# Both merge gates as seven-product groups, with gates and projections behind both attentions, in a two-layer decoder trunk

## The chip, the cores and the metric

The kernel runs on one core of one Trainium2 chip. The metric is the device time of one execution of the whole program, in microseconds (us); lower is better. Engines are named as the profile names them: PE multiplies matrices (PEld is its weight load), DVE is the vector engine, ACT the scalar engine, POOL the GpSimd engine, and SP issues the weight transfers. Three timed executions of the kernel before took 1797.25, 1796.99 and 1792.23 us.

## The reference

Two layers (DEPTH = 2) act on x of 512 tokens by 1024 features, all in float32. Cut to what matters here:

```python
proj = x @ w_in[l]
(r_q, r_k, r_v, r_g, m_qk, m_v, m_o, m_i, m_f, g_a, g_b) = jnp.split(proj, IN_OFFSETS, axis=-1)
o_ret = _head_norm(_retention(rq, rk, rv), ret_norm_g[l]) * jax.nn.silu(r_g.astype(f32))
y_ret = o_ret.astype(dt) @ w_proj_ret[l]
o_ml = _head_norm(_mlstm(mq, mk, mv, i_pre, f_pre), mlstm_norm_g[l]) * jax.nn.sigmoid(m_o.astype(f32))
y_ml = o_ml.astype(dt) @ w_proj_mlstm[l]
gate_a = jax.nn.sigmoid(g_a + b_merge[l, :D_MODEL])
gate_b = jax.nn.sigmoid(g_b + b_merge[l, D_MODEL:])
mix = (gate_a * y_ret + gate_b * y_ml) @ w_out[l]
x = _layer_norm(DEEPNORM_ALPHA * x + mix, ln1_g[l], ln1_b[l])
gu = x @ w_gate_up[l]
hidden = jax.nn.silu(gu[..., :D_FF]) * gu[..., D_FF:]
x = _layer_norm(DEEPNORM_ALPHA * x + hidden @ w_down[l], ln2_g[l], ln2_b[l])
```

The two merge gates, g_a and g_b, are two products of the 512 x 1024 input with 1024 x 1024 weights. The two projections have the same size.

## The kernel before, in words

**Arithmetic.** Every float32 operand is split into a high part and a low part (`whi` and `wlo` of a weight, `x0h` and `x0l` of the input), and every product is made of three matmuls: high x high, high x low, low x high. ACT casts the high part of a weight (`hi_to`, L205), DVE subtracts to get the low part (`lo_of`, L137).

**Weights.** All weights come in units of 128 x 1024 numbers in the order that `layer_plan` (L54) lists. SP loads them into a ring of five raw buffers; the high and low parts have rings of five (`NRING`). After a unit has been used, `used` prepares the units up to four ahead (`LOOK`).

**Units.** A feature unit (`feat`, L270) gives 128 output features for all 512 tokens: 8 blocks of the contraction by 3 parts, 24 matmuls of 512 columns. A token unit (`tok_units`, L359) gives 512 features by blocks of 128 tokens.

**Seven-product groups.** `quad` (L302) computes 2 x 128 output features twice (four units) by Strassen-Winograd: seven products in place of eight, on blocks of half the contraction by half the tokens. A group has 7 x 2 x 4 x 3 = 168 matmuls of 256 columns. It needs four sums of input blocks (tiles `sh`, `sl`; `s0h` in the profile) and four sums of weight blocks (three on DVE in `sum_to`, L191 to L195, one on POOL, L227). The products are called p1, p3, p5, p7, p6, p2, p4, in this order, and go to PSUM banks a, e, c, d (main) and b (auxiliary). Some banks are copied out and then added to again. Before the change only the feed-forward stage uses groups, ten in a layer.

**Order of stages in a layer.** Retention for two pairs of heads; gate A (8 feature units); projection A (8 feature units); mLSTM for two pairs of heads; gate B (8 units); projection B (8 units), mixed with the first branch; output projection; LayerNorm; feed-forward up, then down; LayerNorm.

**Side work.** The attention of a pair of heads (`scores`, `weighted`) and the norm of its outputs (`head_norms`, L515) are generators in the queue `side`. The main stream of matmuls calls `slot` at fixed places, and each call runs one step of the side work, so that small matmuls and transposes stand between large ones. `drain` runs what is left.

**Order on the engines.** PE and SP run in the order in which the code is written. ACT, DVE and POOL are ordered by a scheduler, except in the stretch of the feed-forward groups, where they too follow the code. Every engine runs its own instructions strictly in its order.

**Buffers.** The tag `sc` has four scratch buffers. The tags `qk`, `tab`, `oo`, `vh`, `vl`, `gt`, `pp` hold one tile each at a time. Two pairs of large buffers (`bigpair`) alternate: one holds the layer's input, the other (`oth`) holds the head outputs, `or0h` and `or0l` for retention, then `om0h` and `om0l` for mLSTM (0 is the layer). Projection A's result goes to DRAM (`yd`) and comes back as `ya`.

Of the kernel before, what the change touches and what calls it, by code (L numbers as in the profile page):

```python
# [15 lines left out]
P = 128  # L16
# [37 lines left out]
def layer_plan():  # L54
# [20 lines left out]
    for m in range(8):  # L75
        feat("in", O_GA + m * P)
    for m in range(8):
        feat("ret", m * P)
# [6 lines left out]
    for m in range(8):  # L85
        feat("in", O_GB + m * P)
    for m in range(8):
        feat("ml", m * P)
# [15 lines left out]
QUADS = [layer_plan().index(("F", "gu", j * P)) for j in range(2, FT, 2)]  # L104
# [4 lines left out]
def decoder_trunk(ctx: ExitStack, tc: tile.TileContext, wall, xT_in, x_in, pvec, lnp, rtab, out):  # L109
# [405 lines left out]
    def head_norms(oo, p, gt, gain, oTh, oTl):  # L515
# [22 lines left out]
        for hh in range(2):  # L538
            for f in range(2):
                m = 2 * (2 * p + hh) + f  # L540
# [6 lines left out]
                yield  # L547

# [4 lines left out]
    for l in range(L):  # L553
# [7 lines left out]
        oTh, oTl = bigpair(oth, f"or{l}")  # L561
# [62 lines left out]
        for p in range(2):  # L624
# [29 lines left out]
            side.append(scores(qk, 0, boxes[0], *ret_weights(2 * p)))  # L654
            if p == 0:
                side.append(rest(12))
                side.append(if_cols())
# [28 lines left out]
            side.append(head_norms(oo, p, gt, gain, oTh, oTl))  # L686

        sgs = [reg.tile([P, 4, S], F32, tag="qk", name="sga0"), reg.tile([P, 4, S], F32, tag="tab", name="sga1")]

        def gate_evac(m, base):  # L690
            def ev(pm):
                nc.scalar.activation(sgs[m // 4][:, m % 4], pm, AF.Sigmoid, bias=pv[:, C_BM + base + m : C_BM + base + m + 1])
            return ev

        for m in range(8):
            feat(xh, xl, gate_evac(m, 0))
        drain()
        yd = dr.tile([2, P, 4, S], F32, tag="yd", name="yd")

        def ya_evac(m):  # L700
            def ev(pm):
                s = sgs[m // 4][:, m % 4]
                nc.vector.tensor_tensor(out=s, in0=pm, in1=s, op=ALU.mult)
                if m % 4 == 3:
                    nc.gpsimd.dma_start(yd[m // 4], sgs[m // 4])
            return ev

        for m in range(8):
            feat(oTh, oTl, ya_evac(m))

        oTh, oTl = bigpair(oth, f"om{l}")
# [20 lines left out]
        for p in range(2):  # L732
# [68 lines left out]
            side.append(head_norms(oo, p, gt, gain, oTh, oTl))  # L801


        sgs = [reg.tile([P, 4, S], F32, tag="qk", name="sgb0"), reg.tile([P, 4, S], F32, tag="tab", name="sgb1")]
        for m in range(8):
            feat(xh, xl, gate_evac(m, 8))
        drain()
        yas = [reg.tile([P, 4, S], F32, tag="vh", name="ya0"), reg.tile([P, 4, S], F32, tag="vl", name="ya1")]
        for i in range(2):
            nc.gpsimd.dma_start(yas[i], yd[i])  # L810
        xr = []
        for b in range(NB):
# [3 lines left out]
        gb = reg.tile([P, 2, DM], F32, tag="pp", name="gb1")  # L816
        nc.gpsimd.dma_start(gb, lnp[l, 0:2].unsqueeze(0).broadcast_to([P, 2, DM]))
        mxh, mxl = bigpair(cur, f"mx{l}")

        def mix_evac(m):  # L820
            def ev(pm):
                s = sgs[m // 4][:, m % 4]
# [6 lines left out]
        for m in range(8):  # L829
            feat(oTh, oTl, mix_evac(m))  # L830
# [293 lines left out]
```

## Time and profile before

| | |
|---|---|
| three timed executions | 1797.25, 1796.99, 1792.23 us (median 1796.99) |
| the profiled execution, its own time | 1793.49 us |
| its span in the profile | 1791.8 us |
| mean granted PE clock | 0.998 |
| bytes moved by DMA | 200.95 MB, 112 GB/s on average |
| gate stages of layer 0 in the trace | gate A about 172.6 to 216.1 us, gate B about 414.5 to 458 us |
| feed-forward groups of layer 0 in the trace | 572.6 to 774 us |

The profile is of one execution. Its page lists the busy time of each engine, the span in 40 equal slices with a digit for the busy share, the DMA queues, the chain of work that ended last, and the costliest groups of instructions. From the trace behind it come further views: busy time by stretch of time, instructions in order of time, groups by line, and who waited for whom. A matmul's listed duration includes the time to drain, so matmuls overlap in the list; what one costs in a stream is the distance from its start to the next start. The lines that the argument uses stand with it below.

### The profile page before, as it was taken

What the parts mean: (1) busy time and instruction counts of PE and PEld (TensorE: products, weight loads), DVE (VectorE), ACT (ScalarE), POOL (GpSimd) and SP (SyncE); (2) the same over time, 40 slices, a digit from 0 to 9 for tenths busy, and PEclk for the clock granted to TensorE, in tenths of its full rate; (3) what the DMA queues carried; (4) which work ended last, traced back from release to release, by engine and by line L of the source; (5) the groups of instructions that cost most, each with busy time, mean ns of one, the idle gap of its engine ahead of it and who ended that gap; (6) DMA issues with size and microseconds to landing.
All of it is one profiled execution on the core that took longest, in us unless ns stands there. A gap on an engine that the chain in (4) does not pass through costs nothing.

```text
span 1791.8 us, 24875 instructions
## 1 busy us (share of the span) xinstructions
PE 1778.2 (99%) x10040; PEld 1559.8 (87%) x10040; DVE 1144.4 (64%) x1582; ACT 741.9 (41%) x1056; POOL 327.9 (18%) x245
## 2 busy tenths in 40 slices
PE   9999999999999999999999999999999999999998
PEld 7888888888889999988898888888888899999886
DVE  6665236664459999963476542467535599999534
ACT  4435326554316444451244343256442254444410
POOL 2020000010001455620120100010000015554200
PEclk9999999999999999999999999999999999999999
DMA  7322343234332333363242222522442232333621
GB/s 248 94 83 71 95 148 111 83 115 167 95 95 89 124 95 99 105 216 98 83 165 85 92 82 88 167 87 71 141 153 94 95 107 95 107 115 105 205 71 47
DMA packets 65267, 200.95 MB, mean 112 GB/s; under 512 B 6232, under 2 KB 8152, under 8 KB 63104
## 3 DMA queue, kind: packets, MB, share of 16 engines
q1 hardware_dynamic: 58768, 168.32, 29.3%
q0 software_dynamic: 6384, 31.04, 4.9%
q8 instruction: 79, 1.29, 0.3%
q14 instruction: 36, 0.29, 0.1%
HBM read 186.73 MB, written 12.60 MB: 111 GB/s over the span
## 4 chain that ended last, share of the span: by engine, by line
PE 97%; DVE 1%; ACT 0%; issue 0%; DMA 0%; SPq 0%; DVEq 0%
PE pm L322 19%; PE pm L264 10%; PE pm L266 10%; PE pm L265 10%; PE pm L355 9%; PE pm L357 9%; PE pm L356 9%; PE pa L322 3%; PE pa L356 3%; PE pa L355 3%; PE pa L357 3%; PE pa L488 1%; PE pa L489 1%; PE pa L490 1%; PE pa L543 1%; PE pa L462 1%
## 5 line engine op out<-in xcount | busy, mean ns | idle before, releaser
L137 DVE TENSOR_TENSOR wlo<-wraw,whi 128x1024 fp32r<-128x1024 f32 (+2 forms) x380 | 533.2, 1414 | 347.1 <-ACT whi L205 344.3
L205 ACT CAST whi<-wraw 128x1024 fp32r<-128x1024 f32 x367 | 384.5, 1050 | 616.1 <-PE pm L265 224.8
L444 POOL TENSOR_TENSOR rs<-ve,nhalf 128x4 f32<-128x4 f32 (+1 forms) x32 | 32.1, 1003 | 643.7 <-DVE ve L443 643.7
L264 PE MATMUL pm<-x20h,whi 128*128 128x512 f32 (+1 forms) x288 | 106.9, 371 | 0.0
L266 PE MATMUL pm<-x20h,wlo 128*128 128x512 f32 (+1 forms) x288 | 105.4, 366 | 0.0
L265 PE MATMUL pm<-x20l,whi 128*128 128x512 f32 (+1 forms) x288 | 105.3, 366 | 0.0
L355 PE MATMUL pm<-whi,x0h 128*128 128x512 f32 x256 | 102.3, 400 | 1.8 <-DVE rvl L137 1.7
L355 PE MATMUL pm<-whi,x20h 128*128 128x512 f32 x256 | 102.3, 400 | 0.6 <-DVE rvl L137 0.6
L357 PE MATMUL pm<-wlo,x20h 128*128 128x512 f32 x256 | 100.3, 392 | 0.0
L357 PE MATMUL pm<-wlo,x0h 128*128 128x512 f32 x256 | 100.3, 392 | 0.0
L356 PE MATMUL pm<-whi,x20l 128*128 128x512 f32 x256 | 100.0, 391 | 0.0
L356 PE MATMUL pm<-whi,x0l 128*128 128x512 f32 x256 | 100.0, 391 | 0.0
L264 PE MATMUL pm<-x0h,whi 128*128 128x512 f32 x232 | 91.8, 396 | 0.0
L266 PE MATMUL pm<-x0h,wlo 128*128 128x512 f32 x232 | 90.4, 390 | 0.0
L265 PE MATMUL pm<-x0l,whi 128*128 128x512 f32 x232 | 90.3, 389 | 0.0
L975 POOL TENSOR_TENSOR qa<-qa 128x512 f32<-128x512 f32 x20 | 42.8, 2140 | 142.6 <-DVE qa L974 90.6
L322 PE MATMUL pm<-x10h,whi 128*128 128x256 f32 x240 | 67.9, 283 | 0.0
L322 PE MATMUL pm<-x10l,whi 128*128 128x256 f32 x240 | 67.9, 283 | 0.0
L322 PE MATMUL pm<-s0h,whi 128*128 128x256 f32 x240 | 67.9, 283 | 0.0
L322 PE MATMUL pm<-s0l,whi 128*128 128x256 f32 x240 | 67.9, 283 | 0.0
L322 PE MATMUL pm<-s0h,wlo 128*128 128x256 f32 x240 | 67.9, 283 | 0.0
L322 PE MATMUL pm<-x11h,whi 128*128 128x256 f32 x240 | 67.9, 283 | 0.0
(452 smaller groups left out, 4969.2 us busy)
## 6 DMA issues: line engine op xcount, KB each, us to landing
wraw<-wall SPq DMA_DIRECT2D x307, 512.0 KB, 3.6
yd<-sga POOLq DMA_DIRECT2D x4, 1024.0 KB, 5.0
ya<-yd POOLq DMA_DIRECT2D x4, 1024.0 KB, 6.1
gb<-lnp POOLq DMA_DIRECT2D x4, 1024.0 KB, 5.1
x1d<-xr POOLq DMA_DIRECT2D x8, 512.0 KB, 3.0
xr<-x1d POOLq DMA_DIRECT2D x8, 512.0 KB, 4.6
negm<-md POOLq DMA_DIRECT2D x2, 1026.0 KB, 6.7
xr<-xtok POOLq DMA_DIRECT2D x4, 512.0 KB, 4.0
```

Of the source, the lines that this page charges most:

```text
L137: nc.vector.tensor_tensor(out=out_lo, in0=full, in1=hi.bitcast(F32), op=ALU.subtract)
L205: nc.scalar.copy(hi, sum_t[i])
L264: nc.tensor.matmul(pm[:, c0:c1], lhsT=hi[:, k], rhs=xh[:, k, c0:c1], start=(k == 0), stop=False)
L265: nc.tensor.matmul(pm[:, c0:c1], lhsT=hi[:, k], rhs=xl[:, k, c0:c1], start=False, stop=False)
L266: nc.tensor.matmul(pm[:, c0:c1], lhsT=lo[:, k], rhs=xh[:, k, c0:c1], start=False, stop=(k == KT - 1))
L322: nc.tensor.matmul(pm, lhsT=x[:, j, k], rhs=y[:, k], start=go and n == 0, stop=j == 1 and k == 3 and n == 2, skip_group_check=not first)
L355: nc.tensor.matmul(pm, lhsT=sh(k)[:, a], rhs=hi[:, j], start=first, stop=False)
L356: nc.tensor.matmul(pm, lhsT=sl(k)[:, a], rhs=hi[:, j], start=False, stop=False)
L357: nc.tensor.matmul(pm, lhsT=sh(k)[:, a], rhs=lo[:, j], start=False, stop=last)
L444: nc.gpsimd.tensor_tensor(out=rs[:, :n], in0=ve[:, :n], in1=nhalf[:, :n], op=ALU.pow)
L462: nc.tensor.matmul(pa[:, :HC], lhsT=k[:, t0:t1], rhs=q[:, t0:t2], start=True, stop=True)
L975: nc.gpsimd.tensor_tensor(out=v, in0=v, in1=u, op=ALU.subtract)
```

## The change

It has five parts.

1. **The gates become groups.** Each gate stage is two groups (`quad`) in place of eight feature units. `gate_ev` takes the products out of the banks. Inside the stretch of the four gate groups ACT, DVE and POOL follow the order of the code.
2. **The order of stages** becomes retention, mLSTM, gate A, gate B, projection A, projection B with the mix. `layer_plan` lists the weights accordingly.
3. **Head outputs go through DRAM.** `head_norms` scales a head's two transposed blocks on ACT into a scratch tile `ot`, without splitting it, and POOL's queue stores it to `od`. `fetch`, side work, loads the four blocks of 128 x 1024 later, casts the high part on ACT (`orh`, `om0h`) and subtracts the low part on DVE (`orl`, `om0l`). The retention outputs are fetched during gate B's groups, the mLSTM outputs during projection A.
4. **The four input sums** of the groups (`xs0h`, `xs0l`) are made once per layer by `input_sums`, as side work of the second retention pair, and kept in the large buffers that held the head outputs.
5. **`yd` and `ya` are gone**; gate A's tiles are multiplied by projection A's result in place and stay in SBUF. The `gb1` load follows projection B.

The diff, cut to its core:

```diff
+QUADS = [layer_plan().index(("F", w, c + j * P)) for w, c, js in (("in", O_GA, (0, 4)), ("in", O_GB, (0, 4)),
+                                                                  ("gu", 0, range(2, FT, 2))) for j in js]
...
-    def head_norms(oo, p, gt, gain, oTh, oTl):
+    def head_norms(oo, p, gt, gain, od):
...
+            m = 2 * (2 * p + hh)
+            t = scratch([P, 2, S], "ot")
             for f in range(2):
...
-                nc.scalar.activation(oTh[:, m], pa, AF.Copy, scale=gain[:, m : m + 1])
-                nc.vector.scalar_tensor_tensor(out=oTl[:, m], in0=pa, scalar=gain[:, m : m + 1],
-                                               in1=oTh[:, m].bitcast(F32), op0=ALU.mult, op1=ALU.subtract)
+                nc.scalar.activation(t[:, f], pa, AF.Copy, scale=gain[:, m + f : m + f + 1])
                 yield
+            nc.gpsimd.dma_start(od[:, m : m + 2], t)
+            yield
+
+    def fetch(od, his, los):
+        for i in range(4):
+            t = scratch([P, 2, S], "of")
+            nc.gpsimd.dma_start(t, od[:, 2 * i : 2 * i + 2])
+            yield
+            yield
+            hi, lo = (x[i // 2][:, 2 * i % 4 : 2 * i % 4 + 2] for x in (his, los))
+            nc.scalar.copy(hi, t)
+            yield
+            lo_of(lo, t, hi)
+            yield
+
+    def input_sums(xh, xl, sh, sl):
+        t1, t2 = slice(0, S // 2), slice(S // 2, S)
+        for m in range(4):
+            t = scratch([P, 2, S], "xs")
+            for i in range(2):
+                nc.gpsimd.tensor_tensor(out=t[:, i], in0=xh[:, m + 4 * i].bitcast(F32), in1=xl[:, m + 4 * i].bitcast(F32), op=ALU.add)
+            yield
...
+            nc.scalar.copy(sh[:, :, m], f)
+            lo_of(sl[:, :, m], f, sh[:, :, m])
+            yield
...
+        def gate_ev(sg, base, m):
...
+            def ev(name, banks):
+                two = lambda n: t.setdefault(n, scratch([P, 2, S], n))
+                if name == "p1":
+                    nc.scalar.copy(two("ga")[:, 0], banks["a"])
+                elif name == "p5":
+                    nc.scalar.copy(two("ga")[:, 1], banks["c"])
+                elif name == "p7":
+                    nc.vector.tensor_tensor(out=two("gc")[:, 1], in0=t["ga"][:, 1], in1=banks["d"], op=ALU.subtract)
+                elif name == "p6":
+                    u, v = t["ga"][:, 0], t["ga"][:, 1]
+                    nc.vector.tensor_tensor(out=u, in0=banks["b"], in1=u, op=ALU.add)
+                    nc.gpsimd.tensor_tensor(out=v, in0=v, in1=u, op=ALU.subtract)
+                    nc.gpsimd.tensor_tensor(out=t["gc"][:, 1], in0=t["gc"][:, 1], in1=u, op=ALU.subtract)
+                elif name == "p2":
+                    sigmoid(banks["a"], 0, 0)
+                    nc.vector.tensor_tensor(out=t["gc"][:, 0], in0=banks["e"], in1=t["ga"][:, 1], op=ALU.add)
+                elif name == "p4":
+                    nc.vector.tensor_tensor(out=t["ga"][:, 1], in0=banks["d"], in1=t["ga"][:, 0], op=ALU.add)
...
+        with tc.manual_schedule(engines=ordered):
+            for m in (0, 4):
+                quad(xh, xl, *xs, gate_ev(sga, 0, m))
+            drain()
+            orh = [reg.tile([P, 4, S], F32R, tag=t, name="orh") for t in ("vh", "vl")]
+            orl = [reg.tile([P, 4, S], F32R, tag=t, name="orl") for t in ("gt", "oo")]
+            side.append(fetch(od[0], orh, orl))
+            for m in (0, 4):
+                quad(xh, xl, *xs, gate_ev(sgb, 8, m))
+            drain()
...
+        omh, oml = bigpair(oth, f"om{l}")
+        side.append(fetch(od[1], [omh[:, :4], omh[:, 4:]], [oml[:, :4], oml[:, 4:]]))
         for m in range(8):
+            feat(Halves(orh), Halves(orl), ya_evac(m))
```

How the order of instructions changes, at three places of layer 0. Line numbers of the changed kernel are some lines off from those of the kernel before, as the diff inserts and removes lines.

PE, start of gate A. Before, one feature unit is 24 matmuls of 512 columns with the input as moving operand:

```order
L264 MATMUL pm<-x0h,whi 128x512
L265 MATMUL pm<-x0l,whi 128x512
L266 MATMUL pm<-x0h,wlo 128x512
L264 MATMUL pm<-x0h,whi 128x512
L265 MATMUL pm<-x0l,whi 128x512
L266 MATMUL pm<-x0h,wlo 128x512
```

With the change, the last token unit of the mLSTM (L353) is followed by the first product of a group, of 256 columns each:

```order
L353 MATMUL pm<-wlo,x0h 128x512
L318 MATMUL pm<-x0h,whi 128x256
L318 MATMUL pm<-x0l,whi 128x256
L318 MATMUL pm<-x0h,wlo 128x256
L318 MATMUL pm<-x0h,whi 128x256
L318 MATMUL pm<-x0l,whi 128x256
L318 MATMUL pm<-x0h,wlo 128x256
```

The matmuls have half the columns, and a stage has 336 of them in place of 192.

ACT, first group of gate B in the changed kernel: `ga` holds products taken from a bank, L201 is the cast of a weight's high part, `of` is a fetched block of the head outputs.

```order
L839 COPY ga<-pm 128x512
L201 CAST whi<-wraw 128x1024
L554 CAST orh<-of 128x1024
L201 CAST whi<-wraw 128x1024
L841 COPY ga<-pm 128x512
L201 CAST whi<-wraw 128x1024
L554 CAST orh<-of 128x1024
L201 CAST whi<-wraw 128x1024 x2
L554 CAST orh<-of 128x1024
L833 ACTIVATE sgb<-pm,pv_98 128x256 x2
```

The casts of fetched blocks stand between the casts of weights and the copies out of banks; before, gate B had no such casts, and one sigmoid per unit stood between the weight casts.

POOL, the same place and the second group: L223 is the sum of weight blocks, L847 and L848 combine products, L550 are the loads of head outputs.

```order
L223 TENSOR_TENSOR wraw<-wraw 128x1024
L550 DMA of<-od 128x1024 x3
L847 TENSOR_TENSOR ga<-ga 128x512
L848 TENSOR_TENSOR gc<-gc,ga 128x512
L550 DMA of<-od 128x1024
L223 TENSOR_TENSOR wraw<-wraw 128x1024
L550 DMA of<-od 128x1024 x2
L847 TENSOR_TENSOR ga<-ga 128x512
L848 TENSOR_TENSOR gc<-gc,ga 128x512
L550 DMA of<-od 128x1024 x2
```

The first load stands right behind the sum of weight blocks of the first group, and the fourth behind the two combining operations; the mLSTM outputs' loads follow in the second group.

More of the change, by code (lines that the diff above doesn't have):

```diff
@@ L84, in layer_plan @@
         tok("in", O_MO + p * 512, k8)
[L85 to L88, printed above, removed]
+    for w, col in (("in", O_GA), ("in", O_GB), ("ret", 0), ("ml", 0)):
+        for m in range(8):
+            feat(w, col + m * P)
     for c in range(2):
@@ L560, in decoder_trunk @@
             nc.gpsimd.dma_start(tab, rtab)
-        oTh, oTl = bigpair(oth, f"or{l}")
+        xs = sum_views(oth, f"xs{l}")
+        od = [dr.tile([P, KT, S], F32, tag=f"od{i}", name="od") for i in range(2)]
         def rot_evac(dst):
@@ L685, in decoder_trunk @@
             gain = pv[:, C_RG : C_RG + 8]
[L686 to L711, printed above, removed]
+            side.append(head_norms(oo, p, gt, gain, od[0]))
         negm = reg.tile([P, NH, S + 1], F32, tag="tab", name="negm")
@@ L800, in decoder_trunk @@
             gain = pv[:, C_MG : C_MG + 8]
-            side.append(head_norms(oo, p, gt, gain, oTh, oTl))
-        sgs = [reg.tile([P, 4, S], F32, tag="qk", name="sgb0"), reg.tile([P, 4, S], F32, tag="tab", name="sgb1")]
+            side.append(head_norms(oo, p, gt, gain, od[1]))
+        tab = reg.tile([P, 6, S], F32, tag="tab", name="sg_tab")
+        sga0, sgb0 = reg.tile([P, 4, S], F32, tag="qk", name="sga"), reg.tile([P, 6, S], F32, tag="pp", name="sgb")
+        sga = [(sga0[:, m] if m < 4 else tab[:, m - 4]) for m in range(8)]
@@ L983, in quad_ev @@
             return ev
[L985 removed]
+        with tc.manual_schedule(engines=ordered):
             for j in range(2, FT, 2):
```

56 lines of the change are left out of this document (39 added, 17 removed).

## The prediction

> **What bounds the kernel now.** I read the page first: busy times, slices, and the chain that ended last.
>
> ```profile
> PE 1778.2 (99%) x10040; PEld 1559.8 (87%) x10040; DVE 1144.4 (64%) x1582; ACT 741.9 (41%) x1056; POOL 327.9 (18%) x245
> ...
> PE   9999999999999999999999999999999999999998
> ...
> DVE  6665236664459999963476542467535599999534
> ...
> PEclk9999999999999999999999999999999999999999
> ...
> PE 97%; DVE 1%; ACT 0%; issue 0%; DMA 0%; SPq 0%; DVEq 0%
> ```
>
> PE is busy in every slice, its clock is granted in full, and 97% of the last chain is PE. Of 1791.8 us it is idle for 13.6, mostly at the two ends. So a stage costs the number of its matmuls by the distance between their starts, and the change can win only by that sum. The second thing to see is DVE: it averages 64%, but fills whole slices in the feed-forward groups, and the change puts more such groups into the layer.
>
> Next, who PE waited for:
>
> ```profile
> PE pm L355 <- DVE rvl L137: 2.3, 2, 1.7
> PE pm L399 <- DVE nhalf L401: 1.1, 1, 1.1
> ```
>
> 2.3 us in two waits behind the first attention and 1.1 us at the start: nothing there to win, and any new wait shows at once.
>
> Distances come from the chain in order of time, first for feature units (projection A), then for feed-forward groups:
>
> ```profile
> 204.92 0.23 PE pm L265
> ...
> 207.64 0.23 PE pm L265
> ...
> 572.75 11.52 PE pm L322 x96
> 584.27 2.88 PE pa L322 x24
> 587.15 17.28 PE pm L322 x144
> ```
>
> L265 comes once in three matmuls, and between these two rows it is four threes: 2.72 us / 12 = 0.2267 us for 512 columns. In groups, 11.52 / 96 = 0.1200 us for 256 columns. Half the columns cost 0.53 of the time, not half.
>
> **The change part by part.**
>
> *Gates as groups.* Before, four units take 4 x 24 x 0.2267 = 21.76 us. A group takes 168 x 0.1200 = 20.16 us. One eighth of the products goes, but the smaller matmuls take back half of that, and 1.60 us is left. Two gates in two layers are eight groups: **-12.8 us**. The side transposes that stood between gate units stand between products now, in the same number.
>
> Trainium skill, "TensorE: Matmul & The Clock Gate", section Back-to-back issue gap: a lone warm matmul is followed by the next after its columns / 2.4 plus 2.5 ns, that is 216 ns for 512 columns and 109 ns for 256. By that estimate a group would win 2.4 us and eight would win 19. Both rows above are longer, by 11 ns each, and the same 11 ns on 168 matmuls cost more than on 96; the measured rows decide, so this is not given a chance.
>
> *Retention outputs as moving operand.* They are read from other buffers now: high parts from `vh` and `vl`, low parts from `gt` and `oo`. Tiles of those tags are matmul operands in the down projection:
>
> ```profile
> L264 PE MATMUL pm<-or0h,whi 128*128 128x512 f32 x64 | 24.9, 389 | 0.0
> ...
> L355 PE MATMUL pm<-whi,hd_gt 128*128 128x512 f32 x16 | 6.5, 405 | 0.0
> ...
> L357 PE MATMUL pm<-wlo,hd_oo 128*128 128x512 f32 x16 | 6.3, 391 | 0.0
> ```
>
> Same shape, 2 to 16 ns longer, but there the tile is the stationary operand. For 2 x 192 matmuls in projection A, 0 ns (the present 389) to 6 ns (the common difference) makes 0 to 2.3 us. I take 4 ns, **+1.5 us**.
>
> *Order of stages.* The gates between retention and mLSTM used to give DVE and ACT a rest. The norm of retention's second pair now falls on the mLSTM's first convolution. The trace has that pairing, the first mLSTM pair's norm on the second convolution:
>
> ```profile
> 345.00:358.00 13.00, 13.00 (x67) 10.78 (x66) 10.97 (x16) 6.66 (x10) 0.00 (x0) 1.00 0.36 117
> ```
>
> PE is busy for 13.00 of 13.00 us with DVE at 10.97. The norm also loses its DVE subtraction (L545). Cost nothing; if that cover fails, about the 2.3 us of waits that the first attention has.
>
> *Input sums.* Eight POOL additions of some 2.1 us and their DVE, ACT work lie in the second retention pair, 150 us before their use. Nothing. `yd`, `ya`, `od`: a transfer in DRAM more or less is hidden, except where an engine waits for it in its order, which comes now.
>
> *Gate groups on DVE.* The timeline of one feed-forward group, which starts on PE at 653.2 us (DVE, POOL, ACT):
>
> ```profile
> 655.62 7.58 DVE L137 TENSOR_TENSOR wlo<-wraw,whi 128x1024 fp32r<-128x1024 f32 x3
> ...
> 666.69 1.22 DVE L137 TENSOR_TENSOR wlo<-wraw,whi 128x1024 fp32r<-128x1024 f32 x1
> ...
> 671.81 0.68 DVE L979 TENSOR_TENSOR qb<-pm,qa 128x512 f32<-128x512 f32 x1
> ```
>
> ```profile
> 655.23 2.41 POOL L227 TENSOR_TENSOR wraw<-wraw 128x1024 f32<-128x1024 f32 x1 [2.35 <-issue]
> 657.59 4.53 POOL L957 TENSOR_TENSOR hf_gt<-qb,qc 128x512 f32<-128x512 f32 x2
> ```
>
> ```profile
> 592.90:754.20 161.30, 161.30 (x1347) 161.30 (x1346) 155.90 (x114) 75.28 (x89) 89.09 (x40) 1.00 0.34 105
> ```
>
> DVE is busy 155.9 / 8 = 19.5 us of each 20.16. A subtraction takes 1.22 us alone; three beside 6.94 us of POOL work take 7.58, so DVE loses about (7.58 - 3.66) / 6.94 = 0.56 us per us of POOL. A gate group lacks the POOL products (4.53), so it has about 19.5 - 2.5 = 17.0 us of DVE.
>
> In gate A's first group the norm's work joins: for the second head four statistics, and eight multiplications.
>
> ```profile
> L529 DVE SCALAR_TENSOR_TENSOR moo<-moo,mv,mgt 128x256 f32<-128x256 f32 x32 | 15.1, 476 | 1.4 <-ACT mgt L796 1.4
> L521 DVE BATCH_NORM_STATS2 st<-moo 128x6 f32<-128x256 f32 x32 | 13.2, 422 | 9.4 <-ACT moo L786 9.4
> ```
>
> 4 x 0.42 + 8 x 0.48 = 5.5 us, early, where four weight units lie prepared and no bank is due for DVE until p7 ends at 4 x 2.88 = 11.5 us. With four subtractions (4.9, beside POOL 6.2) DVE is done at about 11.7. Nothing.
>
> In gate B the fetch joins: four casts on ACT, four subtractions on DVE, each in order. The loads are of 512 KB from DRAM, like this one:
>
> ```profile
> xr<-x1d POOLq DMA_DIRECT2D x8, 512.0 KB, 4.6
> ```
>
> The first stands on POOL's queue behind the sum L227, which ends 4.4 us into a group (655.23 + 2.41 - 653.2); landed 4.6 later, 9.0. Until then ACT stands at the cast (1.05 us, as for a weight of that size) and DVE at its subtraction. DVE has had one weight to do by then, until about 4.7, and goes on at 10.05: **5.3 us lost**. Queued behind it are the weights of p2 and p4 and the copies out of the banks. The weights still come in time: p2 starts at 14.4, its low part follows the fetched one at 10.05 + 1.22 + 1.22 = 12.5. The banks don't: the last one from DVE in a group (bank e, at p2) is now free at 19.3 (671.81 + 0.68 - 653.2), and PE needs it in the next group's p3, at 20.16 + 2.88 = 23.0: 3.7 us of slack. Up to there DVE is later by 5.3 + 3 x 1.22 = 9.0, less the 2.5 us of POOL contention and 0.7 us of idle time: 5.8. So PE waits 5.8 - 3.7 = **2.1 us a layer**, +4.2 in two. Bounds: nothing, if the load lands 2 us earlier; 7 us a layer, if a second load holds DVE for its whole 4.6 us and more.
>
> In gate B's second group DVE catches up: no weight sums follow there, 3 x 1.22 less.
>
> Trainium skill, "SBUF — State Buffer", section Who interferes with whom: DVE with two SBUF inputs and a GpSimd read exclude each other for a whole instruction. The rows agree in direction, not in size: 3.9 us are lost beside 6.9. By full exclusion the two POOL operations of p6, 4.4 us, would cost DVE 4.4 in place of 2.5 us, and the wait would be 2 us longer in each layer. The rows' share is in the sum.
>
> **Sum.** -12.8 + 1.5 + 4.2 = -7.1 us, against the profiled execution's own 1793.49 us (span 1791.8 and 1.7 around it): 1786.4. The runs shown have their median 3.5 us above that execution, and all four average 1795.0, 1.5 above. I put the forecast there: **1788.0 us**.
>
> **Rivals.**
>
> *No wait in gate B.* For it: the lead of four prepared units, and feed-forward groups run with PE at 161.30 of 161.30. Against it: the queue places above. With projection A at 389 ns, -12.8: about 1781.
>
> *A second load waits in full.* The third and the fourth stand behind work that itself waits for DVE. 4.6 us and 0.6 of issue more in each layer, +10.4: -7.1 + 10.4 = +3.3, about 1797: no change.
>
> *Every fetched block holds ACT and DVE (slower).* The place is the same, the mechanism is order: the next load can only be issued when a scratch buffer comes free, buffers come free when DVE subtracts, and DVE waits for the load before. Three more waits of 5.2 us in each layer are 31 us: 1786.4 + 31 = 1817.5. For it: `sc` has four buffers and `ga`, `gc` need two of them. Against it: the first two loads are issued together, so each has two buffers to turn in. It decides slower from a wait of 8.4 us a layer: 2 x 8.4 + 1.5 - 12.8 = +5.5.
>
> That the change doesn't do what it says is out: the groups stand on PE, 1344 matmuls of 256 columns in place of 768.
>
> **How the numbers follow.** Forecast 0.50, no wait 0.25, a second load 0.15, every block 0.10. The range leaves out the last alone and takes the bounds: from -12.8 on the fastest run, 1792.23, so 1779.5, to the second load with the four executions' average, 1795.0 + 3.3, so 1798.5. About 0.3% is what a measurement of this kernel can tell from no change, 5.4 us. The forecast crosses that line when the wait exceeds 3 us a layer; I give a third of its chance to that, 0.17. Faster: 0.33 + 0.25 = 0.58. Same: 0.17 + 0.15 = 0.32. Slower: 0.10.
>
> **What would show it.** Gate groups of 20.16 us on PE, with one gap in each layer: at the start of gate B's second group, before its first or second product, ended by DVE or ACT. ACT idle before the first cast of `orh` until a DMA, some 4 us. Projection A's matmuls at 389 to 395 ns. No PE idle time in gate A or the mLSTM's first convolution. Wrong would be: several idle stretches of ACT before `orh` or `om0h` for a DMA, PE waiting in gate A for the norms, or distances in the gate groups off 0.120 us.

## The result, and the profile after

| | before | changed kernel |
|---|---|---|
| executions | 1797.25, 1796.99, 1792.23, 1796.80 us | 1806.10, 1805.87, 1808.64, 1808.35 us |
| median | 1796.89 us | 1807.22 us |
| ratio, 95% interval | | 1.0064 (1.0044 to 1.0083) |
| profiled execution, span | 1793.49 us, 1791.8 us | 1806.10 us, 1804.4 us |

The change makes the kernel slower by 0.64%, outside the predicted range of 1779.5 to 1798.5 us. The page of the changed kernel: busy times, slices of PE, DVE and PE's clock, and the chain that ended last.

```profile
PE 1772.4 (98%) x10616; PEld 1580.5 (88%) x10616; DVE 1263.8 (70%) x1686; ACT 794.3 (44%) x1148; POOL 420.6 (23%) x309
...
PE   9998999999999999999999999999999999999997
...
DVE  6676666775459999963476856667755599999534
...
PEclk9999999999999999999999999999999999999999
...
PE 92%; DVE 5%; issue 1%; ACT 1%; DMA 1%; POOL 0%; SPq 0%; DVEq 0%; ACTq 0%
```

PE is busy for 5.8 us less than before, and yet the span is 12.6 us longer: PE's idle time grew by 18.4 us. One slice of PE is down to 8, the fourth, 135 to 180 us; the chain now holds 5% of DVE. The waits of PE (what PE ran next, whom it waited for, us in total, times, longest):

```profile
PE pm L351 <- DVE rvl L133: 15.1, 4, 6.4
PE pa L318 <- DVE wlo L133: 2.8, 2, 1.7
```

The first row had 2.3 us in two waits before. Now it has 15.1 in four. L351 is a token unit, and `rvl` is the low part of retention's values that DVE copies out of PSUM. The second row is new: gate groups (L318) that wait for a weight's low part.

All stages were compared by the starts of their first matmuls. (By these starts gate A of the kernel before runs from 170.7 to 216.1 us and gate B from 413.6 to 459.0, so each begins one to two us earlier than the table ahead of the prediction says.) A values stage here holds retention's values and its output gates. The ledger of the span, in us:

| where | before | changed | difference, both layers |
|---|---|---|---|
| start, to the first feature unit | 26.42 | 27.45 | +1.0 |
| second values stage of retention, layers 0 and 1 | 54.29, 54.29 | 62.26, 63.26 | **+16.9** |
| gates A and B with the convolution that took a norm over, without waits | 45.41 + 45.39 + 21.76 | 82.37 + 23.65 | -13.1 |
| waits in gate B | 0 | 1.31, 2.38 | +3.7 |
| projection A, each layer | 43.52 | 44.53 | +2.0 |
| down projection of layer 1 to the end of the span | 129.26 | 131.12 | +1.9 |
| the rest | | | +0.2 |
| sum | | | 12.6 |

(82.37 us is what two gate stages take in the run with the longer lead below, where PE does not wait.) In the chain in order of time, a gate group on PE is 24 x 7 matmuls of 0.1200 us, as forecast, until the last group of gate B:

```profile
372.04 17.28 PE pm L318 x144
389.32 2.88 PE pa L318 x24
392.20 17.29 PE pm L318 x144
409.50 1.23 DVE wlo L133
410.77 2.90 PE pa L318 x22
```

Here 17.28 + 2.88 = 20.16 us is one group, and 409.50 is the wait, at the group's fifth product (p6).

**The large term.** Windows of the changed kernel (busy PE, PEld, DVE, ACT, POOL, each with its instructions, then PE's granted clock, DMA share, GB/s). First the values stage up to PE's stop, the stop, and the matmuls behind it:

```profile
117.50:140.60 23.10, 23.10 (x106) 19.21 (x105) 22.61 (x29) 7.20 (x10) 14.46 (x9) 1.00 0.22 71
140.60:147.40 6.80, 0.42 (x3) 0.01 (x1) 6.80 (x11) 4.96 (x7) 0.00 (x0) 0.72 0.36 98
...
147.39:150.11 2.72, 2.72 (x6) 2.14 (x7) 2.72 (x4) 0.97 (x2) 0.00 (x0) 0.50 0.36 142
```

The same stretch before the change:

```profile
116.40:139.30 22.90, 22.90 (x105) 19.01 (x104) 11.80 (x20) 7.81 (x12) 2.32 (x1) 1.00 0.33 108
```

DVE went from 11.80 to 22.61 us, full, and stays full in the next 6.80 us, for 6.38 of which PE stands. The groups of DVE and POOL between 117.5 and 147.4 us (busy, mean ns, idle before):

```profile
L583 DVE TENSOR_TENSOR sf<-xs 128x256 f32<-128x256 f32 x8 | 6.5, 825 | 0.0
L133 DVE TENSOR_TENSOR xs0l<-sf,xs0h 128x1024 fp32r<-128x1024 f32 x4 | 6.0, 1494 | 0.0
L583 DVE TENSOR_TENSOR sf<-sf,xs 128x256 f32<-128x256 f32 x8 | 5.5, 689 | 0.1
...
L577 POOL TENSOR_TENSOR xs<-x0h,x0l 128x512 f32<-128x512 f32 x8 | 12.2, 1539 | 5.5 <-DVE sf L583 2.6 <-DVE xs0l L133 2.0 <-DVE pp L133 0.8
```

These are the input sums: 18.0 us of DVE. What PE needs stands behind them, as DVE's timeline shows:

```profile
138.60 1.51 DVE L583 TENSOR_TENSOR sf<-sf,xs 128x256 f32<-128x256 f32 x1
140.04 0.41 DVE L583 TENSOR_TENSOR sf<-xs 128x256 f32<-128x256 f32 x1
...
145.50 1.23 DVE L133 TENSOR_TENSOR xs0l<-sf,xs0h 128x1024 fp32r<-128x1024 f32 x1
146.65 1.88 DVE L133 TENSOR_TENSOR rvl<-pm,rvh 128x512 fp32r<-128x512 f32 x3
```

```profile
147.39 0.79 PE L351 MATMUL pm<-whi,x0h 128*128 128x512 f32 x1 [6.38 <-DVE rvl L133]
```

The four main banks hold the values until `rvl` has been read out of them, and the gate units of retention that follow need those banks. The copies wait in DVE's order for the last sum, which ends at about 146.7. The row at 138.60 shows the other half: a subtraction that takes 0.41 us alone takes 1.51 beside an addition on POOL.

### The profile page after: what moved, and what is told of

Its sections match the earlier page's. It is cut to its first block, busy times and chain, and to the rows that moved or that the text cites. A ratio compares the mean times of both kernels' runs of the same rounds, so it can differ in the third digit from the quotient of the medians.

```text
span 1804.4 us, 26440 instructions
## 1 busy us (share of the span) xinstructions
PE 1772.4 (98%) x10616; PEld 1580.5 (88%) x10616; DVE 1263.8 (70%) x1686; ACT 794.3 (44%) x1148; POOL 420.6 (23%) x309
## 4 chain that ended last, share of the span: by engine, by line
PE 92%; DVE 5%; issue 1%; ACT 1%; DMA 1%; POOL 0%; SPq 0%; DVEq 0%; ACTq 0%
PE pm L318 25%; PE pm L351 9%; PE pm L352 8%; PE pm L353 8%; PE pm L262 7%; PE pm L260 7%; PE pm L261 7%; PE pa L318 4%; PE pa L352 3%; PE pa L351 3%; PE pa L353 3%; DVE wlo L133 1%; DVE sf L583 1%; PE pa L484 1%; PE pa L485 1%; PE pa L486 1%
## 5 line engine op out<-in xcount | busy, mean ns | idle before, releaser
L133 DVE TENSOR_TENSOR wlo<-wraw,whi 128x1024 fp32r<-128x1024 f32 (+2 forms) x404 | 569.8, 1423 | 231.3 <-ACT whi L201 228.8
L201 ACT CAST whi<-wraw 128x1024 fp32r<-128x1024 f32 x391 | 408.8, 1049 | 507.2 <-PE pm L261 133.9
L351 PE MATMUL pm<-whi,x0h 128*128 128x512 f32 x256 | 102.9, 402 | 8.2 <-DVE rvl L133 8.1
L351 PE MATMUL pm<-whi,x20h 128*128 128x512 f32 x256 | 103.2, 403 | 7.0 <-DVE rvl L133 7.0
L353 PE MATMUL pm<-wlo,x20h 128*128 128x512 f32 x256 | 100.9, 394 | 0.0
L353 PE MATMUL pm<-wlo,x0h 128*128 128x512 f32 x256 | 100.7, 393 | 0.0
L223 POOL TENSOR_TENSOR wraw<-wraw 128x1024 f32<-128x1024 f32 x28 | 67.4, 2408 | 110.1 <-issue 54.4
L318 PE MATMUL pm<-s1h,wlo 128*128 128x256 f32 x240 | 67.9, 283 | 0.0
L318 PE MATMUL pm<-x10h,whi 128*128 128x256 f32 x240 | 67.9, 283 | 0.0
L318 PE MATMUL pm<-x10h,wlo 128*128 128x256 f32 x240 | 67.9, 283 | 0.0
L318 PE MATMUL pm<-s0h,whi 128*128 128x256 f32 x240 | 67.9, 283 | 0.0
L318 PE MATMUL pm<-x11h,whi 128*128 128x256 f32 x240 | 67.9, 283 | 0.0
L318 PE MATMUL pm<-x10l,whi 128*128 128x256 f32 x240 | 67.9, 283 | 0.0
L318 PE MATMUL pm<-s0l,whi 128*128 128x256 f32 x240 | 67.9, 283 | 0.0
L318 PE MATMUL pm<-x11l,whi 128*128 128x256 f32 x240 | 67.9, 283 | 0.0
L318 PE MATMUL pm<-s1h,whi 128*128 128x256 f32 x240 | 67.9, 283 | 0.0
L318 PE MATMUL pm<-s0h,wlo 128*128 128x256 f32 x240 | 67.9, 283 | 0.0
L318 PE MATMUL pm<-x11h,wlo 128*128 128x256 f32 x240 | 67.9, 283 | 0.0
```

What stands on the lines that cost most here:

```text
L133: nc.vector.tensor_tensor(out=out_lo, in0=full, in1=hi.bitcast(F32), op=ALU.subtract)
L201: nc.scalar.copy(hi, sum_t[i])
L223: nc.gpsimd.tensor_tensor(out=raw_t[u + 2], in0=raw_t[u], in1=raw_t[u + 3], op=ALU.add)
L318: nc.tensor.matmul(pm, lhsT=x[:, j, k], rhs=y[:, k], start=go and n == 0, stop=j == 1 and k == 3 and n == 2, skip_group_check=not first)
L351: nc.tensor.matmul(pm, lhsT=sh(k)[:, a], rhs=hi[:, j], start=first, stop=False)
L353: nc.tensor.matmul(pm, lhsT=sh(k)[:, a], rhs=lo[:, j], start=False, stop=last)
```

## The experiments

Ratios are against the kernel before on the same chip: 1796.89 us for the changed kernel, medians of 1794.08 and 1793.85 us in the two sets of experiments. The last two rows have one execution each, and the kernel before had one beside them, of 1793.42 us; for them the time stands in place of the ratio, and only their stages are used. Stage lengths, from the starts of their first matmuls in the profiled executions, in us, layers 0 and 1:

| | ratio (95%) | values stage | two gate stages | projection A | down, layer 0 | down, layer 1, to the end |
|---|---|---|---|---|---|---|
| changed kernel | 1.0064 (1.0044 to 1.0083) | 62.26, 63.26 | 83.68, 84.75 | 44.53 | 122.98 | 131.12 |
| sums of high parts | 0.9967 (0.9954 to 0.9980) | 54.25, 54.25 | 83.81, 85.05 | 44.53 | 122.98 | 131.12 |
| sums spread | 0.9959 (0.9944 to 0.9974) | 54.23, 54.23 | 83.62, 84.48 | 44.53 | 122.98 | 131.12 |
| longer lead | 1.0041 (1.0026 to 1.0056) | 63.63, 63.01 | 82.37, 82.36 | 44.53 | 122.98 | 131.12 |
| padding to 128 B | 1.0038 (1.0023 to 1.0052) | 62.10, 62.28 | 83.59, 84.79 | 44.30 | 122.41 | 130.66 |
| spread and lead | 0.9955 (0.9942 to 0.9967) | 54.23, 54.23 | 82.38, 82.38 | 44.53 | 122.98 | 131.12 |
| and padding to 256 B | 0.9926 (0.9914 to 0.9938) | 54.07, 54.07 | 82.36, 82.36 | 43.55 | 121.51 | 129.64 |
| and stores by SP | 0.9911 (0.9897 to 0.9924) | 54.07, 54.07 | 82.36, 82.36 | 43.55 | 121.51 | 128.35 |
| before, padding to 256 B | 0.9975 (0.9966 to 0.9985) | 54.13, 54.13 | | 43.52 | 121.51 | 127.78 |
| spread, lead of first block | 1803.16 us | 54.23, 54.23 | 91.94, 91.35 | 44.53 | 122.98 | 131.13 |
| spread, lead of last block | 1784.08 us | 54.23, 54.23 | 82.38, 83.19 | 44.53 | 122.98 | 131.13 |

### Sums without POOL's additions

```diff
-            t = scratch([P, 2, S], "xs")
-            for i in range(2):
-                nc.gpsimd.tensor_tensor(out=t[:, i], in0=xh[:, m + 4 * i].bitcast(F32), in1=xl[:, m + 4 * i].bitcast(F32), op=ALU.add)
...
-            a11, a12, a21, a22 = t[:, 0, t1], t[:, 1, t1], t[:, 0, t2], t[:, 1, t2]
+            a11, a12, a21, a22 = (xh[:, m + 4 * i, h].bitcast(F32) for h in (t1, t2) for i in range(2))
```

> The input sums are made from the high parts of the input alone: POOL's eight additions per layer go, DVE's subtractions, ACT's casts and their places stay (the result loses the low part of the input in the summed blocks). Theory LOAD: in the second retention pair the sums are 18.0 us of DVE, 6.4 us of it stretched by POOL's additions; without them DVE has 11.8 + 11.6 = 23.4 us to do in a stage of 23, so PE's wait behind the v units falls from 6.5 us to at most 1 us in each layer, no half-clock matmuls follow, and the time is 1790 to 1794 us. Theory ORDER: the sums stand ahead of the copies out of the v banks on ACT and DVE, each cast waiting for a subtraction, and that chain sets the wait whatever POOL does: a wait of 3.5 us or more stays in each layer and the time is 1799 us or more.

Measured 1788.82 us, ratio 0.9967, a little under the 1790 to 1794 us that LOAD gave; the values stages are back at 54.25. The window and DVE's two groups of sums in it:

```profile
116.82:139.72 22.90, 22.90 (x106) 19.03 (x105) 21.35 (x40) 11.72 (x16) 2.31 (x1) 1.00 0.36 113
...
L580 DVE TENSOR_TENSOR sf<-sf,x0h 128x256 f32<-128x256 f32 x8 | 3.3, 415 | 0.0
L580 DVE TENSOR_TENSOR sf<-x0h 128x256 f32<-128x256 f32 x8 | 3.2, 414 | 0.0
```

The same sixteen instructions, all still ahead of the copies out of the banks, take 6.5 us in place of 12.0, and DVE just fits, with 21.35 of 22.90 us. So the place in the queue alone is not the cause; ORDER falls. The sums and POOL's part in stretching them together overfill the stage.

### Sums spread over four stages

```diff
-            if p == 1:
-                side.append(input_sums(xh, xl, *xs))
...
-            side.append(rest(2))
+            side.append(input_sums(xh, xl, *xs, [p]))
...
-            side.append(rest(2))
+            side.append(input_sums(xh, xl, *xs, [2 + p]))
```

(The first replaced `rest(2)` is in retention's stage of the output gates, the second in the mLSTM's; the new argument lists the blocks to sum.)

> The same sums, a quarter in each of the four stages with gate units of the attentions (31 us each, DVE busy 17 of 31 there before) in place of the two empty steps of the side work. Theory LOAD: some 4.5 us of DVE more per stage fits; no PE wait in any attention, stage lengths as in the kernel before; the 8.0 and 9.0 us that the second retention pair's v stage has over the kernel before go: 1807.2 - 16.9 = 1790.3 us, range 1788 to 1794. Rival PLACE: additions on POOL hurt wherever they stand (the norms' small POOL operations and DVE's chain wait behind them): PE waits of 1 us or more in several of the eight stages, 1797 us or more.

Measured 1787.44 us, ratio 0.9959; LOAD's 1788 to 1794 us were worked out from the first set of runs, in which the kernel before was 2.8 us slower. All the work is done, POOL's too, and no stage is longer for it. This version is faster than the kernel before: what the gates win is real, and the sums hid it.

### A longer lead for the fetched blocks

```diff
-            yield
-            yield
+            for _ in range(4):
+                yield
```

> Only the fetch is changed: four steps in place of two lie between a block's load and its cast. Theory LANDING: ACT and DVE stand 3.0 and 4.3 us for the first fetched block in gate B, and that lag comes out as PE's wait in p6 of gate B's second group (1.2 us in layer 0, 1.9 in layer 1, with 0.4 at its second group's start); with the lead these go: 3.4 us less, 1803.8 us (1802 to 1805.5), ACT's idle time for a DMA before orh under 0.5 us. Rival AMOUNT: gate B has 17 + 5 = 22 us of DVE per 20.16 us group, and the wait stays within 0.7 us in each layer: 1806 to 1808 us.

Measured 1802.56 us, ratio 1.0041, and both gate stages at 82.4. DVE's two waits in gate B of layer 0, in the changed kernel:

```profile
387.47 1.23 DVE L133 TENSOR_TENSOR orl<-of,orh 128x1024 fp32r<-128x1024 f32 x1 [4.34 <-ACT orh L554]
...
408.36 1.23 DVE L133 TENSOR_TENSOR orl<-of,orh 128x1024 fp32r<-128x1024 f32 x1 [3.02 <-ACT orh L554]
```

With the lead:

```profile
388.17 1.23 DVE L133 TENSOR_TENSOR orl<-of,orh 128x1024 fp32r<-128x1024 f32 x1 [2.78 <-ACT orh L554]
...
413.58 1.22 DVE L133 TENSOR_TENSOR orl<-of,orh 128x1024 fp32r<-128x1024 f32 x1
```

The idle time at the first block falls from 4.34 to 2.78 us and that at the fourth from 3.02 to nothing; 1.20 us now stand before the third. PE's wait is gone. The fourth block comes late in the changed kernel for a reason that POOL's timeline shows: its load stands behind the combining of products.

```profile
396.85 4.42 POOL L847 TENSOR_TENSOR ga<-ga 128x512 f32<-128x512 f32 x1 [7.33 <-ACT whi L201]
401.23 1.29 POOL L848 TENSOR_TENSOR gc<-gc,ga 128x512 f32<-128x512 f32 x1
402.46 0.56 POOL L550 DMA_DIRECT2D of<-od  x1
```

LANDING holds in time and stages, though ACT still stands 1.73 us before the first cast of `orh`, where it had given under 0.5. This run does not tell which block PE felt. The last two runs do.

### Padding to 128 B

```diff
-    NPP = O_ST + 2 * (DV + 2)
+    NPP = O_ST + 2 * (DV + 2) + 28
...
-            vh = reg.tile([P, NB, 2, DV + 2], F32R, tag="vh", name="mvh")
+            vh = reg.tile([P, NB, 2, DV + 4], F32R, tag="vh", name="mvh")
```

(`vl` likewise; `weighted` reads as many columns as before.)

> Only padding: mLSTM's v tiles 64 bytes longer, the attention's work tile 112 bytes longer, so that the tiles that share these buffers (orh, orl, hd_vl, hd_gt, the v tiles) all start 96 bytes past a multiple of 128, as x0h and s0h do; before, vl started at 32 and gt at 0. Theory ADDRESS: projection A's 5.3 ns per matmul over 226.7 come from mixing starts; its stage returns from 44.53 to 43.5 us (2.0 us in two layers), and the down projection, 528 matmuls in 122.98 us, comes to about 120 us (528 x 0.2267 = 119.7): 5 to 6 us in two layers; 1798 to 1801 us in all. Rival SWITCH: the extra time comes with every change of operand tile, wherever it starts: no stage changes by more than 0.2 us, 1806 to 1808.5 us.

Measured 1801.63 us, ratio 1.0038. Neither theory fits: projection A went from 44.53 to 44.30, not to 43.5. One tile did move all the way, `pp`, before and after the padding:

```profile
L351 PE MATMUL pm<-whi,hd_pp 128*128 128x512 f32 x24 | 9.5, 396 | 0.0
```

```profile
L351 PE MATMUL pm<-whi,hd_pp 128*128 128x512 f32 x24 | 9.3, 389 | 0.0
```

Its start had moved by 128 B, to a multiple of 256 B from the start of the weight ring; `vl` and `gt` had moved by 64 and 224 B, to 128 and 384 B off, and stayed slow. (The tiles' starts follow from their sizes in the kernel.) So the next padding went to 256 B.

### Both mends together

> The changed kernel with the input sums a quarter at a time in the four stages of the output gates (as in the run that spread them) and with four steps in place of two between the load and the cast of a fetched block (as in the run with the longer lead). LANDING says that the wait in gate B comes from ACT and DVE standing at a block that has not landed, and that it does not depend on what the sums did before: the two gate stages, 83.62 and 84.48 us from the first to the last PE start in the run that only spread, come to 82.4 each as in the run that only had the lead, 3.3 us together, so the span goes from 1785.0 to 1781.7 and the ratio from 0.9959 to about 0.9940. DVE-LIMIT says that the gate groups are short of DVE time whatever the lead, and that the lead helped only because DVE stood elsewhere in that run: the stages stay at 83.5 or more, no ratio under 0.9955.

Measured 1785.00 us, ratio 0.9955: the stages are those that LANDING gives, 82.38 both. The ratio is not the 0.9940 that was worked out from the stages, and its interval meets that of the spread alone; this profiled execution spent 4.0 us more than the spread run's ahead of its second stage of feature units (95.98 against 91.93 us). That is the granted clock: here it was 0.50 from 12.22 to 19.04 and from 63.42 to 66.83 us, with 9.5 us of PE work in these stretches; in the spread run's execution it was 1.00 from 4.72 us until behind the last matmul. The last section shows the second stretch.

### Padding to 256 B

```diff
-    NPP = O_ST + 2 * (DV + 2)
+    NPP = O_ST + 2 * (DV + 2) + 60
...
-            vh = reg.tile([P, NB, 2, DV + 2], F32R, tag="vh", name="mvh")
+            vh = reg.tile([P, NB, 2, DV + 8], F32R, tag="vh", name="mvh")
```

> The kernel before this one in the list, with padding behind the mLSTM's values (6 more elements for each head and block) and behind the table of its weights (60 elements), so that all tiles that feed a matmul start a multiple of 256 B from each other. In the run that padded to 128 B, 227 ns between matmuls came with the tiles whose distance from the weight ring is a multiple of 256 B (pp, which the padding had moved by 128 B, and vh), 231 to 239 ns with those at 64, 128, 160 or 384 B off a multiple. STEP-256 says the residue decides: projection A goes from 44.53 to about 43.6 us in each layer (2 x 0.95), the down projection of layer 0 from 122.98 to about 120.5 (2 x 2.4 in both layers), the attention stages lose some 0.1 us each as before; 6 to 8 us in all, span about 1775. TRAFFIC says that it is what other engines and transfers do in SBUF at that time: projection A stays above 44.2, the down projection above 122.2, and the span falls by no more than the 2.8 us of the padding to 128 B.

Measured 1781.20 us, ratio 0.9926, span 6.3 us less. Projection A's groups in the changed kernel and here (mean ns last but one):

```profile
L261 PE MATMUL pm<-orl,whi 128*128 128x512 f32 x128 | 50.6, 395 | 0.0
L260 PE MATMUL pm<-orh,whi 128*128 128x512 f32 x128 | 50.5, 394 | 0.0
```

```profile
L261 PE MATMUL pm<-orl,whi 128*128 128x512 f32 x128 | 49.8, 389 | 0.0
L260 PE MATMUL pm<-orh,whi 128*128 128x512 f32 x128 | 49.8, 389 | 0.0
```

Projection A is at 43.55, as fast as the projection that reads the old buffers. STEP-256 holds there in full. The down projection lost 1.47 us and not the 2.4 that were expected, but its matmuls too now follow each other at 226 to 228 ns, whatever tile they read: 528 x 0.2267 = 119.7 us, and the other 1.8 us are 16 transposes that stand between them at 0.11 us each. The expectation had left these out.

### The same padding on the kernel before

> The kernel before the change with the padding to 256 B alone. STEP-256 says that its down projections (121.0 to 123 us) lose some 2.4 us each and its attention stages 0.1 us each: 5 to 6 us, ratio about 0.997, with no change in the projections on retention's outputs, which read tiles that stand right already. TRAFFIC says no more than 0.999 to 1.001.

Measured 1788.39 us, ratio 0.9975: both down projections lose 1.47 us, the attention stages 0.1 to 0.2 each. TRAFFIC's 0.999 to 1.001 is out. So 0.25% of the best version's gain belongs to the padding and not to the change; with the padding in both, change and mends make 1781.20 / 1788.39 = 0.9960.

### The end of the program

```diff
-            nc.gpsimd.dma_start(od[:, m : m + 2], t)
+            nc.sync.dma_start(od[:, m : m + 2], t)
```

> The kernel before this one in the list, with the 16 stores of the head outputs issued on SyncE's queue in place of POOL's. The program ends with a drain on POOL, which took 5.04 us in the kernel before with 49 transfers issued on POOL and 7.00 us in the changed one with 73; it ends last of all engines there. DRAIN says that it grows with the number of transfers, 1.96 us / 24 = 0.08 us each: with 57 it takes 7.00 - 16 x 0.082 = 5.7 us, and the end from the last matmul on is 1.3 us shorter. FIXED says that the length has another cause: it stays at 7.0. HELD says that SyncE, which issues its transfers in order, stands at a store until ACT has written the block, and that weights behind it come late: new PE waits in the attention stages, span longer than in the kernel before this one by more than 1 us.

Measured 1777.59 us, ratio 0.9911 (0.9897 to 0.9924), the fastest version. The drains of POOL at the program's end (ns: shortest, median, longest) before the change, after it, and with the stores on SP:

```profile
L1120 POOLq DRAIN  x3: 45/102/5041, 1785.9 to 1791.5; - x3
```

```profile
L1194 POOLq DRAIN  x3: 45/93/7001, 1796.6 to 1804.1; - x3
```

```profile
L1192 POOLq DRAIN  x3: 45/102/5696, 1769.4 to 1775.6; - x3
```

POOL issues 49, 73 and 57 transfers in the three. From 73 to 49 the drain loses 1.960 us, from 73 to 57 1.305: 0.082 us for each, both times. DRAIN's 5.7 us came out, and no new wait on PE with it. The end is 1.3 us shorter; the rest of the 3.6 us between the two medians is not the store's, as the profiled executions differ by 2.3 us ahead of the second stage of feature units, with the clock at 0.50 for 3.4 us there in place of 10.2.

### Which block is felt

```diff
-            yield
-            yield
+            for _ in range(4 if i == 0 else 2):
+                yield
```

> The kernel that spreads the sums, with four steps in place of two between load and cast for the first block of a fetch alone. Which of the two stands of DVE does PE feel in gate B: the one at the first block (4.3 us idle before its low part in the changed kernel) or the one at the fourth (3.0 us), whose load POOL issues late and right behind which PE waits? FIRST-BLOCK says that the time lost at the first is what makes DVE late for all that follows: with it shortened the two gate stages take 82.4 us as with the long lead on all four. FOURTH-BLOCK says that they stay near 83.6 and 84.5 us. BOTH says that each adds its part: something between, near 83.0 and 83.4.

The other run has `i == 3`.

> The same with four steps for the fourth block alone. FOURTH-BLOCK: the two gate stages take 82.4 us. FIRST-BLOCK: they stay near 83.6 and 84.5. BOTH: between, near 83.0 and 83.4.

With the lead on the fourth alone, layer 0 is at 82.38 and layer 1 at 83.19: FOURTH-BLOCK, all of layer 0's 1.24 us and 1.29 of layer 1's 2.1. The other 0.8 us of layer 1 are waits at p2 and p4 of its last group; their cause stays open. With the lead on the first alone the stages went to 91.94 and 91.35, which no theory had said. PE's waits in that run, and DVE's two at the third and fourth block:

```profile
PE pm L318 <- DVE wlo L133: 6.4, 2, 4.0
PE pm L318 <- DVE ga L851: 5.7, 2, 3.2
```

```profile
397.33 1.23 DVE L133 TENSOR_TENSOR orl<-of,orh 128x1024 fp32r<-128x1024 f32 x1 [4.69 <-ACT orh L554]
...
408.25 1.23 DVE L133 TENSOR_TENSOR orl<-of,orh 128x1024 fp32r<-128x1024 f32 x1 [4.86 <-ACT orh L554]
```

POOL's rows say why: the third and the fourth load now stand right behind other work on POOL's queue, with two steps left to their casts.

```profile
390.27 1.29 POOL L846 TENSOR_TENSOR gc<-gc,ga 128x512 f32<-128x512 f32 x1
391.50 0.56 POOL L550 DMA_DIRECT2D of<-od  x1
399.93 2.39 POOL L223 TENSOR_TENSOR wraw<-wraw 128x1024 f32<-128x1024 f32 x1 [7.86 <-issue]
402.26 1.09 POOL L550 DMA_DIRECT2D of<-od  x2
```

Two more steps for the first block move all later blocks by two steps. What counts is where in the group a load falls, not how early the first one is.

## Why the prediction was wrong

**Input sums, "Nothing": wrong, +16.9 us, the step that failed.** The prediction looked at when the sums are used, 150 us later, and so put them at nothing. It did not add them up on DVE in the stage in which they run, and the row for that was in the trace of the kernel before: 11.80 us of 22.90. Sixteen instructions of 0.42 us and four of 1.22 make 11.6, so 23.4 alone; beside 12.2 us of POOL additions, at the prediction's own 0.56 us lost per us of POOL, 6.8 more. By this estimate, made afterwards, there are 30.2 us of DVE in 22.9, and PE stops for 7.3; the trace has 6.4 in each layer. The rest of the 8.0 and 9.0 us is the clock: the row 147.39:150.11 has PE at 0.50, six matmuls in 2.72 us, twice the usual distance. PE ran at 0.50 for 3.0 us in layer 0 and for 5.2 us in layer 1, half of which was lost, 1.5 and 2.6 us; that also makes the two layers differ.

The Trainium skill, "SBUF — State Buffer", section Who interferes with whom, says that such a DVE instruction and a GpSimd read shut each other out for a whole instruction. The trace agrees, in size too: each of the eight additions held up one DVE instruction, by 0.9 to 1.1 us. Six of these are sums (18.0 us for 11.6 alone) and two are other work of the attention (1.9 us more). The last two additions and what they held up, 1.22 and 0.41 us long alone:

```profile
136.19 3.64 POOL L577 TENSOR_TENSOR xs<-x0h,x0l 128x512 f32<-128x512 f32 x2 [1.96 <-DVE xs0l L133]
```

```profile
136.36 2.32 DVE L133 TENSOR_TENSOR xs0l<-sf,xs0h 128x1024 fp32r<-128x1024 f32 x1
138.60 1.51 DVE L583 TENSOR_TENSOR sf<-sf,xs 128x256 f32<-128x256 f32 x1
```

The listed time of a POOL operation holds its own waiting for DVE: the second addition starts at 137.55 and is listed with 2.28 us, as `xs0l` runs first, while POOL's operations of this shape that nothing holds up take 1.29 us. The prediction took the listed time for POOL's work and so saw agreement in direction but not in size; by 1.29 us each, the two operations of p6 would cost DVE about 2.6 us, next to the 2.5 in its sum.

**Gate groups, -12.8 us: right.** 20.16 us each; -13.1 with the transposes.

**Wait in gate B, 2.1 us a layer: size right in part by luck, block and place wrong.** Measured 1.31 and 2.38. DVE did stand for the first block (4.34 us, against 5.3 forecast), but PE felt the fourth, whose load POOL issued only at 402.46. That is the mechanism of the rival "a second load waits in full"; its price of 5.2 us a layer was too high here, because only PE's p6 in the second group was reached. The gap came at p6, not at the group's first or second product. A time near the slow rival's is one shift of two steps away: in the run with the lead of the first block the gate stages are 9.6 and 9.0 us longer than without waits. There three of the four blocks hold DVE, by their places in POOL's queue and not, as the rival had it, for want of scratch buffers.

**Projection A, +1.5: mis-sized, 2.0.** The matmuls take 393 to 395 ns, near the upper end of the bounds. The cause is the tiles' start, not the buffers' role as an operand: with the padding the same buffers feed at 389 ns.

**Norm beside the mLSTM's first convolution, head norm in gate A: nothing, right.** The convolution takes 23.65 us (21.76 and the transposes), and PE does not wait in gate A.

**Not thought of: the end, +1.9**, POOL's longer drain. The +1.0 at the start lies within what the runs differ by there: their first feature unit starts between 25.45 and 28.10 us, latest where the clock was at 0.50 longest (6.8 us) ahead of it and earliest where it never was, and nothing of the change comes ahead of it.

Without the sums' term the forecast's own terms give -7.1 against the -7.4 that gates, waits and projection A made together. That they agree so closely is in part luck: the three were off by -0.3, -0.5 and +0.5.

## What to carry to other kernels

Work that is needed late is not hidden because it is early: add it to every engine in the stage in which it runs, with what it costs beside a busy neighbour (here about 1 us of DVE for each POOL addition), and look at what stands behind it in that engine's order and holds PSUM banks. On a queue that runs in order, a transfer's price is set by what stands ahead of it and by how many steps lie between it and its first use; move it by whole steps and measure, since one step can turn a small wait into a large one. When the terms add up to less than a per cent, the end of the program and the start addresses of tiles are terms too.

## What the hardware showed that was not expected

- 512-column matmuls follow each other at 226 to 228 ns (listed with 389 to 390) for all tiles of projection A and of the down projection once these tiles start a multiple of 256 B from the weight ring. In the changed kernel the tiles that start elsewhere stand at 229 to 235 ns (listed with 390 to 397). With 256 B padding projection A lost 0.98 us of 44.53. Why 256 B was not tried. One group at `gt` stays at a mean of 400 ns (405 before) for another reason: two of its sixteen matmuls follow transposes and are listed with 476 ns, the others with 389.
- The last drain of POOL took 5.04, 5.70 and 7.00 us with 49, 57 and 73 transfers issued on POOL in the whole program, 0.082 us for each one more.
- PE's granted clock was 0.50 for some us after some of PE's stops and not after others, and the length of the stop does not decide it. A stop of 1.74 us behind the first attention, at about 62 us, stands in all twelve traces; the clock was 0.50 after it in three of them. In the run with the lead of the first block it was 0.50 after stops of 4.01, 3.15 and 2.35 us and stayed at 1.00 after one of 2.52. What decides, as far as the twelve traces show, is where a stop falls. In each trace the clock changes only at points that are a multiple of 3.41 us apart. Where it was 1.00 up to such a point, it was 0.50 behind it if PE had been busy for at most 1.70 of the last 3.41 us, and it stayed if PE had been busy for 1.89 or more; with 1.82 it went each way once. That stop in the run with both mends, cut at these points:

```profile
60.01:63.42 3.41, 1.46 (x10) 0.84 (x8) 3.31 (x7) 1.81 (x3) 0.59 (x2) 1.00 0.02 2
63.42:66.83 3.41, 3.41 (x10) 2.83 (x11) 3.09 (x5) 0.21 (x1) 0.00 (x0) 0.50 0.58 154
```

In the kernel before, where one of the points falls into the stop:

```profile
57.84:61.25 3.41, 1.90 (x11) 1.21 (x9) 3.31 (x6) 2.12 (x3) 1.06 (x2) 1.00 0.16 61
61.25:64.66 3.41, 2.92 (x16) 2.53 (x17) 3.41 (x6) 0.59 (x2) 0.00 (x0) 1.00 0.51 156
```

The points lie elsewhere in each execution, so the same stop can cost one execution more than another: the stage of this stop takes 58.82 and 57.27 us in the two.

The Trainium skill, "TensorE: Matmul & The Clock Gate", section Part 1: The HAM clock gate, gives one idle window of about 3.4 us as the condition for half the clock. The rows agree with the window's length, not with its being idle: PE was busy for 1.46 us of the first one above.
